# Seven products of quarters in the first feed-forward as well

## The chip, the cores and the metric

One NeuronCore of a Trainium2 chip runs the whole program. The metric is the device time of one execution in microseconds. PE is the TensorE engine (PEld its weight loads), DVE VectorE, ACT ScalarE, POOL GpSimd, SP the SyncE engine that issues most DMAs.

## What is computed

One block of a network on 256 tokens of width 2048, all in float32: a feed-forward, a mixer (S5 recurrence beside pooling), attention to a memory of 256 rows, and a second feed-forward. The part of the reference that the change touches is the two feed-forwards; the S5 tables and the norm of the memory only because their work is run beside the first.

```python
def rmsnorm(x, g):
    return x * rsqrt(mean(x * x, axis=-1, keepdims=True) + EPS) * g
def swiglu(x, w_gate, w_up, w_down):                   # 2048 -> 5632 -> 2048
    return (silu(x @ w_gate) * (x @ w_up)) @ w_down

h = h + 0.5 * swiglu(rmsnorm(h, g_ffn1), w1_gate, w1_up, w1_down)
...                                                    # mixer: s5_mixer(u_ssm, a, dt, b, c, ...), pool_mixer
memn = rmsnorm(mem, g_mem)
h = h + memory_cross_attention(rmsnorm(h, g_xattn), memn, w_q, w_k, w_v, w_o)
h = h + 0.5 * swiglu(rmsnorm(h, g_ffn2), w2_gate, w2_up, w2_down)
return rmsnorm(h, g_final)
```

## The kernel before

**Products.** A float32 weight tile is loaded as a 1 MB tile `raw` (128x4x512; pool `wraw`, three slots). `parts` (L137) splits it in two halves of 128x1024: ACT rounds the half to `whi` (L142), DVE subtracts to get `wlo` (L143). A pair of tiles whi and wlo comes from the pool `whl` with three slots; in the second feed-forward every second or third pair comes from another pool with two. The tokens are split in the same way (`xh`, `xl`). `tok_block` (L151 to L158) makes three 128x512 matmuls for each half of the tokens: xh by whi, xh by wlo, xl by whi. So a half-tile of weights feeds twelve matmuls, a tile 24.

**A chunk.** The 5632 inner columns are eleven chunks `f` of 512. A plain chunk is `tok_unit` (L163) over four tiles of gate and four of up, 192 matmuls in all; `gated` (L271) and `upped` (L282) make the product, `act_tiles` (L286) transposes and splits it for the down projection. These last steps are put on a list `late` and run at the next tile.

**The first feed-forward** (`ffn`, L294 to L339) runs the chunks in four passes (`PASSES`, L25), three chunks each and then two; after each pass come its four down tiles in width, each over the pass's chunks, and `add_to_h` (L258). All its chunks are plain. Beside it runs `aside` (L543 on), a generator with the tables of the S5 recurrence (`s5_tables`, L342 to L533: DVE products, PE transposes, writes of `Vd`, `WTd`, `Kd` to DRAM) and the sum of squares of the memory: 16 tiles `mem` of 128x256, each with a one-column memset on DVE (L550), a load that POOL issues (L551), a square on ACT (held in program order), and a sum into `ssm` on DVE (L202); the norm of it (`rnorm` L224, `spread` L215) goes into `Rm`. `step` (L299) advances the generator in five of every nine weight tiles, from the seventh on, so that it lasts through all eleven chunks; `mem` has six buffers.

**The second feed-forward** (L1006 on) runs chunks 0 and 1 plain and chunks 2 to 10 by `seven`: from quarters of the weights and of the tokens, seven products in place of eight. `product` (L1053 to L1062) makes 12 matmuls for a half product, with sums and differences of weight tiles (`less`, DVE operations of 128x512 x 2) and of tokens (`token_sums`: ten sums and differences on DVE, then SH on ACT and SL on DVE, in two `raw` slots). Such a chunk has 84 matmuls in `product` and 96 in `tok_block`, 180 in all, and more work on DVE and ACT than a plain one. Its buffers are in a pool `sw`. The down tiles of a pass are a generator `down`, which the chunks of the next pass advance. The first pass with seven products is pass 1.

What sets the order is program order on each engine; an engine runs its instructions one after the other, and a tile's slot that is not yet free holds the load or the memset that writes it, with all behind it. PSUM has eight banks: in the first feed-forward, the mixer and the attention pools of 6 and 2, in the second feed-forward 4 and 2, and two for the down tiles.

Of the kernel before, what the change touches and what calls it, by code (L numbers as in the profile page):

```python
# [23 lines left out]
PASSES2 = ((0, 2), (2, 4), (4, 6), (6, 8), (8, 10), (10, 11))  # L24
PASSES = ((0, 3), (3, 6), (6, 9), (9, 11))  # L25
# [29 lines left out]
def block_kernel(ctx: ExitStack, tc: tile.TileContext, xT, memT, wgu1, wd1, w_in, w_glu, w_pool, w_out,  # L55
# [10 lines left out]
    banks = ExitStack()  # L66
    psA = banks.enter_context(tc.tile_pool(name="psA", bufs=6, space=bass.MemoryType.PSUM))
    psB = banks.enter_context(tc.tile_pool(name="psB", bufs=2, space=bass.MemoryType.PSUM))
# [225 lines left out]
    def ffn(fe, wgu, wd, xs, aside=None, begin=None, before=None, after=None):  # L294


        calls = [0]

        def step():  # L299
            calls[0] += 1  # L300
            if aside is not None and calls[0] > 6 and calls[0] * 5 % 9 < 5:
                next(aside, None)

        late = []

        def held(more=None):
            def run(i):
                if i == 0:
                    while late:
                        late.pop(0)()  # L310
                if more is not None:
                    more(i)
                step()
            return run

        for a, b in PASSES:
            acts = []
            for f in range(a, b):
                if f == 0 and begin is not None:
                    ag, au = begin()  # L320
                else:
                    ag, au = tok_unit([cols4(wgu[4 * f:4 * f + 4, 0], i) for i in range(4)], xs, held(before if f == 0 else None)), None
                if f == 0:
                    ffn_norm()
                ss = gated(fe, ag)
                if au is None:
                    au = tok_unit([cols4(wgu[4 * f:4 * f + 4, 1], i) for i in range(4)], xs, held())
                upped(ss, au)
                late += [lambda ss=ss, t=t: act_tiles(ss, acts, t) for t in range(2)]
            for n in range(ND):  # L330
                more = None
                if b == FC and after is not None:
                    more = lambda i, n=n: after(n, i)
                add_to_h(tok_unit([cols4(wd[f, 4 * n:4 * n + 4], 0) for f in range(a, b)], acts, held(more)), n, qcol)
                if b == FC:
                    squares(n)
        if aside is not None:
            for _ in aside:
                pass  # L339

# [201 lines left out]
    with tc.tile_pool(name="pp", bufs=1) as pp, tc.tile_pool(name="fe1", bufs=2) as fe:  # L542
# [16 lines left out]
        def begin():  # L559
# [54 lines left out]
        ffn(fe, wgu1, wd1, xs, aside(), begin,  # L614
            after=lambda n, i: layer_in(xm, n - 1, G_MIX, [xp] * KT) if n > 0 and i == 1 else None)
# [393 lines left out]
    banks.close()  # L1009
    psA = ctx.enter_context(tc.tile_pool(name="psC", bufs=4, space=bass.MemoryType.PSUM))  # L1010
    psB = ctx.enter_context(tc.tile_pool(name="psD", bufs=2, space=bass.MemoryType.PSUM))
    fe = ctx.enter_context(tc.tile_pool(name="fe2", bufs=2))
    gate_up = lambda f, m: wgu2[4 * f:4 * f + 4, m]
    late = []

    def flush(n=2):
        for _ in range(min(n, len(late))):
            late.pop(0)()

    def finish_chunk(ss, acts):  # L1020
        late.extend([lambda t=t: act_tiles(ss, acts, t) for t in range(2)])

    def plain(f, acts, before=None):
        def first(i):
            flush()
            if before is not None:
                before(i)

        ag = tok_unit([cols4(gate_up(f, 0), i) for i in range(4)], xf, first)
        if f == 0:  # L1030
            ffn_norm()
        ss = gated(fe, ag, 2)
        upped(ss, tok_unit([cols4(gate_up(f, 1), i) for i in range(4)], xf))
        finish_chunk(ss, acts)

    def down(a, b, acts, accs_of=tok_accs, done=None):

        for n in range(ND):
            accs = accs_of()
            for i, f in enumerate(range(a, b)):  # L1040
                blocks = wtile(cols4(wd2[f, 4 * n:4 * n + 4], 0))
                flush()
                for j, w in enumerate(blocks):
                    tok_block(accs, w, acts[4 * i + j], i + j == 0, f == b - 1 and j == 3)
                if f == b - 1:
                    add_to_h(accs, n, qcol)
                    if done is not None:
                        done(n)
                yield

    def less(out, a, b):
        for c in (0, 256):
            V.tensor_tensor(out=out[:, :, c:c + 256], in0=a[:, :, c:c + 256], in1=b[:, :, c:c + 256], op=ALU.subtract)  # L1053

    def product(acc, w, x, first, last):

        acc = acc.rearrange("p (f c) -> p f c", f=4)
        for j, (wh, wl) in enumerate(parts(w)):
            xh, xl = x(j)
            T.matmul(acc, xh, wh, start=first and j == 0, stop=False)  # L1060
            T.matmul(acc, xh, wl, start=False, stop=False)  # L1061
            T.matmul(acc, xl, wh, start=False, stop=last and j == 3)  # L1062

    def quarter(k, lt):
        return lambda j: [xf[k + j][:, i * L + lt * P:i * L + (lt + 1) * P] for i in range(2)]

    with tc.tile_pool(name="sw", bufs=1) as sw:
        pairs[:] = [whl, sw, whl, sw, whl]
        SH = sw.tile([P, 4, 4, P], F32R, name="SH")
        SL = sw.tile([P, 4, 4, P], F32R, name="SL")  # L1070

        def token_sums():

            x = wraw.tile([P, 8, L], F32, name="raw")
            for k in range(8):
                V.tensor_tensor(out=x[:, k], in0=xf[k][:, :L].bitcast(F32), in1=xf[k][:, L:].bitcast(F32), op=ALU.add)
            q = [[x[:, 4 * i:4 * i + 4, lt * P:(lt + 1) * P] for i in range(2)] for lt in range(2)]
            s = wraw.tile([P, 4, 4, P], F32, name="raw")
            for o, a, b, op in ((0, q[1][0], q[1][1], ALU.add), (1, s[:, 0], q[0][0], ALU.subtract),
                                (2, q[0][0], q[1][0], ALU.subtract), (3, q[0][1], s[:, 1], ALU.subtract)):  # L1080
                V.tensor_tensor(out=s[:, o], in0=a, in1=b, op=op)
            for o in (0, 2):
                S.activation(out=SH[:, o:o + 2], in_=s[:, o:o + 2], func=AF.Copy)
                V.tensor_tensor(out=SL[:, o:o + 2], in0=s[:, o:o + 2], in1=SH[:, o:o + 2].bitcast(F32), op=ALU.subtract)

        def tsum(o):
            return lambda j: (SH[:, o, j], SL[:, o, j])

# [62 lines left out]
        for a, b in PASSES2:  # L1151
            acts = []
            for f in range(a, b):
                if f < 2:
                    plain(f, acts, (lambda i: layer_in(xf, ND - 1, G_FFN2, [xp] * KT) if i == 3 else None) if f == 0 else None)
                    if f == 0:
                        token_sums()
# [111 lines left out]
```

## Time and profile before

| | us |
|---|---|
| three runs | 2136.57, 2137.09, 2141.73 (median 2137.09) |
| profiled execution: its own time | 2138.39 |
| its span on the core | 2136.6 |
| PE busy | 2095.8 (98%) |
| PEld busy | 1731.6 (81%) |
| DVE busy | 1502.9 (70%) |
| ACT busy | 1077.2 (50%) |
| POOL busy | 141.5 (7%) |
| mean granted clock of PE | 0.995 |

The busy shares are means over stages with different limits. Matmuls are pipelined: a row's duration is longer than the distance to the next one. The rows of the trace below name an instruction by its line, engine and operation, the tile that it writes, the tiles that it reads, and the shapes.

### The profile page before, as it was taken

Reading aid. Unit: us, or ns where it says so; the run is one execution under the profiler, and the core shown is the slowest. Engines: PE = TensorE matmul, PEld = TensorE weight load, DVE = VectorE, ACT = ScalarE, POOL = GpSimd, SP = SyncE. Lnnn points to the kernel's source line nnn. Section 1 sums busy time; section 2 is a strip of 40 time slices with the busy share of each in tenths; the row PEclk is TensorE's granted clock in tenths of the full one; section 3 lists DMA queues with packets and bytes.
Section 4 is the critical chain, followed back from the end, with each engine's and each line's share of the span. In section 5 each row is a group of like instructions: output and inputs, shape, how many; then the busy total and the mean of one; then the engine's idle time right before and its main releaser. Section 6 shows DMA issues by size and latency. Waiting matters only on the chain.

```text
span 2136.6 us, 26778 instructions
## 1 busy us (share of the span) xinstructions
PE 2095.8 (98%) x10248; PEld 1731.6 (81%) x10248; DVE 1502.9 (70%) x2021; ACT 1077.2 (50%) x1510; POOL 141.5 (7%) x255
## 2 busy tenths in 40 slices
PE   8999999999999999979999999999999999999997
PEld 7888888888888888867888888888888888888885
DVE  5567776766656667836767755566888888888874
ACT  7443444344444555625655644544555555555553
POOL 0000011111110001840000000000000000000000
PEclk9999999999999999999999999999999999999999
DMA  7755777777776756868545556656665666565542
GB/s 239 216 182 193 214 212 222 215 223 221 217 225 185 233 196 220 263 202 246 190 161 178 196 179 210 203 166 225 181 198 178 193 210 209 181 201 187 183 155 96
DMA packets 202320, 427.58 MB, mean 200 GB/s; under 512 B 17872, under 2 KB 31376, under 8 KB 193104
## 3 DMA queue, kind: packets, MB, share of 16 engines
q1 hardware_dynamic: 181280, 392.35, 58.3%
q0 software_dynamic: 6416, 18.85, 3.0%
q10 hardware_dynamic: 14496, 14.68, 2.2%
q8 instruction: 80, 1.31, 0.2%
q14 instruction: 48, 0.39, 0.0%
HBM read 408.05 MB, written 16.78 MB: 199 GB/s over the span
## 4 chain that ended last, share of the span: by engine, by line
PE 92%; POOL 3%; DMA 2%; DVE 1%; ACT 1%; issue 1%; SPq 0%; DVEq 0%; ACTq 0%; POOLq 0%
PE acc L158 19%; PE acc L156 19%; PE acc L157 19%; PE acc L120 6%; PE dacc L156 3%; PE dacc L157 3%; PE dacc L158 3%; PE acc L121 3%; PE psb L1060 2%; PE psb L1062 2%; PE psb L1061 2%; PE acc L987 1%; PE acc L988 1%; PE acc L986 1%; PE acc L1062 1%; PE acc L1060 1%
## 5 line engine op out<-in xcount | busy, mean ns | idle before, releaser
L143 DVE TENSOR_TENSOR wlo<-raw,whi 128x1024 fp32r<-128x1024 f32 x522 | 636.3, 1224 | 362.7 <-ACT whi L142 357.8
L142 ACT ACTIVATE whi<-raw 128x1024 fp32r<-128x1024 f32 x522 | 553.4, 1061 | 644.8 <-PE acc L158 462.3
L157 PE MATMUL acc<-wlo,x 128*128 128x512 f32 x1760 | 689.7, 392 | 0.0
L158 PE MATMUL acc<-whi,x 128*128 128x512 f32 x1760 | 688.2, 392 | 0.0
L156 PE MATMUL acc<-whi,x 128*128 128x512 f32 x1760 | 637.7, 393 | 0.3 <-DVE h L262 0.3
L158 PEld LDWEIGHTS acc<-whi,x 128*128 128x128 f32 x1760 | 331.0, 188 | 70.6 <-issue 1.2
L157 PEld LDWEIGHTS acc<-wlo,x 128*128 128x128 f32 x1760 | 331.2, 188 | 70.1 <-issue 0.4
L156 PEld LDWEIGHTS acc<-whi,x 128*128 128x128 f32 x1760 | 330.5, 188 | 70.2 <-issue 1.1
L120 PE MATMUL acc<-x,whi 128*128 128x512 f32 x848 | 299.9, 399 | 3.1 <-ACT whi L100 3.1
L101 DVE TENSOR_TENSOR wlo<-raw,whi 128x1024 fp32r<-128x1024 f32 (+1 forms) x144 | 171.9, 1199 | 123.9 <-ACT whi L100 108.1
L121 PE MATMUL acc<-x,wlo 128*128 128x256 f32 x848 | 235.3, 283 | 2.8 <-DVE wlo L101 2.8
L100 ACT ACTIVATE whi<-raw 128x1024 fp32r<-128x1024 f32 (+1 forms) x144 | 146.8, 1023 | 153.5 <-PE acc L120 94.7
L120 PEld LDWEIGHTS acc<-x,whi 128*128 128x128 f32 x848 | 158.5, 188 | 41.4 <-ACT whi L100 5.2
L121 PEld LDWEIGHTS acc<-x,wlo 128*128 128x128 f32 x848 | 159.1, 189 | 8.3 <-DVE wlo L101 5.3
L158 PE MATMUL dacc<-whi,x 128*128 128x512 f32 x320 | 125.8, 394 | 0.0
L156 PE MATMUL dacc<-whi,x 128*128 128x512 f32 x320 | 124.9, 395 | 1.0 <-DVE h L264 1.0
L157 PE MATMUL dacc<-wlo,x 128*128 128x512 f32 x320 | 125.3, 391 | 0.0
L142 ACT ACTIVATE whi<-t 128x1024 fp32r<-128x1024 f32 x54 | 57.4, 1062 | 50.1 <-PE acc L158 30.1
L143 DVE TENSOR_TENSOR wlo<-t,whi 128x1024 fp32r<-128x1024 f32 x54 | 65.0, 1225 | 20.5 <-ACT whi L142 19.5
L143 DVE TENSOR_TENSOR wlo<-r,whi 128x1024 fp32r<-128x1024 f32 x54 | 65.9, 1220 | 15.1 <-ACT whi L142 15.1
L142 ACT ACTIVATE whi<-r 128x1024 fp32r<-128x1024 f32 x54 | 56.2, 1057 | 36.5 <-PE acc L158 15.0
L156 PEld LDWEIGHTS dacc<-whi,x 128*128 128x128 f32 x320 | 60.1, 188 | 14.0 <-issue 1.4
(276 smaller groups left out, 2135.3 us busy)
## 6 DMA issues: line engine op xcount, KB each, us to landing
raw<-in_wgu SPq DMA_DIRECT2D x148, 1024.0 KB, 6.1
raw<-in_wd SPq DMA_DIRECT2D x88, 1024.0 KB, 5.3
r<-in_wgu SPq DMA_DIRECT2D x27, 1024.0 KB, 6.1
raw<-in_w_in SPq DMA_DIRECT2D x16, 1024.0 KB, 5.0
raw<-in_w_k SPq DMA_DIRECT2D x16, 1024.0 KB, 5.3
raw<-in_w_out SPq DMA_DIRECT2D x32, 512.0 KB, 5.1
raw<-in_w_q SPq DMA_DIRECT2D x16, 1024.0 KB, 4.8
raw<-in_w_v SPq DMA_DIRECT2D x16, 1024.0 KB, 4.8
```

The lines of the kernel that those rows point to most:

```text
L100: S.activation(out=hi[:, :n], in_=r, func=AF.Copy)
L101: V.tensor_tensor(out=lo[:, :n], in0=r, in1=hi[:, :n].bitcast(F32), op=ALU.subtract)
L120: T.matmul(acc, w[0], x, start=first, stop=False)
L121: T.matmul(acc[:, :L], w[1], x[:, :L], start=False, stop=last)
L142: S.activation(out=hi, in_=raw[:, :, c:c + 256], func=AF.Copy)
L143: V.tensor_tensor(out=lo, in0=raw[:, :, c:c + 256], in1=hi.bitcast(F32), op=ALU.subtract)
L156: T.matmul(acc, xh, w[0], start=first, stop=False)
L157: T.matmul(acc, xh, w[1], start=False, stop=False)
L158: T.matmul(acc, xl, w[0], start=False, stop=last)
L1060: T.matmul(acc, xh, wh, start=first and j == 0, stop=False)
L1061: T.matmul(acc, xh, wl, start=False, stop=False)
L1062: T.matmul(acc, xl, wh, start=False, stop=last and j == 3)
```

## The change

The functions of the seven products move into `ffn`, which now serves both feed-forwards. In the first, chunks 5 to 10 use them (`SEVEN1`), in the second chunks 1 to 10 (`SEVEN2`). Both use the same passes: one chunk, then five of two chunks. So in the first feed-forward too the down tiles of a pass are run from within the next pass's chunks (`steps`), in accumulators `dacc` of their own, and its PSUM pools are 4 and 2 banks; the mixer and attention get 6 and 2 as before (`open_banks`). The side work `aside` is advanced by `tick` at each weight tile of the plain chunks 1 to 4, once and twice in turn. At chunk 5 `room` runs what is left of it, closes its pool `pp` and opens the pool `sw` of the seven products in the same memory; then come the token sums. In the second feed-forward the token sums stand at chunk 1, no longer within chunk 0. The code of `seven`, `product`, `less` and `token_sums` is the same as before apart from names.

```diff
-PASSES2 = ((0, 2), (2, 4), (4, 6), (6, 8), (8, 10), (10, 11))
-PASSES = ((0, 3), (3, 6), (6, 9), (9, 11))
+PASSES = ((0, 1), (1, 3), (3, 5), (5, 7), (7, 9), (9, 11))
+SEVEN1 = 5
+SEVEN2 = 1
...
+    psA, psB = open_banks(4)
...
+    def ffn(fe, wgu, wd, xs, seven_from, room, begin=None, before=None, tick=None):
+        gate_up = lambda f, m: wgu[4 * f:4 * f + 4, m]
+        todo = [iter(()), 0]
+
+        def steps(slot, slots=4):
+            flush()
+            for _ in range((slot + 1) * todo[1] // slots - slot * todo[1] // slots):
+                next(todo[0], None)
+
+        def plain(f):
+            def ahead(m):
+                def run(i):
+                    if i % 2 == 1 or todo[1] == 0:
+                        steps(2 * m + i // 2)
+                    if before is not None and f == 0 and m == 0:
+                        before(i)
+                    if tick is not None:
+                        tick()
+                return run
...
         for a, b in PASSES:
             acts = []
             for f in range(a, b):
...
+                if f == seven_from:
+                    sw = room()
+                    pairs[:] = [whl, sw, whl, sw, whl]
+                    SH, SL = (sw.tile([P, 4, 4, P], F32R, name=n) for n in ("SH", "SL"))
+                    token_sums()
+                ss = seven(f) if f >= seven_from else plain(f)
+                late.extend([lambda ss=ss, t=t, acts=acts: act_tiles(ss, acts, t) for t in range(2)])
+            for _ in todo[0]:
                 pass
+            if b < FC:
+                todo[0] = down(wd, a, b, acts, lambda: [psA.tile([P, 512], F32, name="dacc", bufs=2) for _ in range(2)])
+                n = next(y - x for x, y in PASSES if x == b)
+                todo[1] = ND * (b - a) // n
...
-        ffn(fe, wgu1, wd1, xs, aside(), begin,
-            after=lambda n, i: layer_in(xm, n - 1, G_MIX, [xp] * KT) if n > 0 and i == 1 else None)
+        def tick():
+            count[0] += 1
+            for _ in range(1 + (count[0] % 2)):
+                next(side, None)
+
+        def room():
+            for _ in side:
+                pass
+            spare.close()
+            return spare.enter_context(tc.tile_pool(name="sw", bufs=1))
+
+        for n, i in ffn(fe, wgu1, wd1, xs, SEVEN1, room, begin, tick=tick):
+            if n > 0 and i == 0:
+                layer_in(xm, n - 1, G_MIX, [xp] * KT)
+        spare.close()
+    psA, psB = open_banks(6)
...
+    units = ffn(fe, wgu2, wd2, xf, SEVEN2, lambda: spare.enter_context(tc.tile_pool(name="sw", bufs=1)),
+                before=lambda i: layer_in(xf, ND - 1, G_FFN2, [xp] * KT) if i == 3 else None)
```

**ACT where the tiles of mem begin.** Before, in the last chunks of the first feed-forward; `kr` is the last of the tables' work, `whi` a split of weights, `ssm` and `evq` the squares of mem.

```order
L529 ACTIVATE kr<-psb 128x128
L142 ACTIVATE whi<-raw 128x1024 x5
L198 ACTIVATE ssm<-mem 128x256
L142 ACTIVATE whi<-raw 128x1024 x4
L198 ACTIVATE evq<-mem 128x256 x2
```

After, at the end of chunk 4 and the entry to chunk 5:

```order
L203 ACTIVATE ssm<-mem 128x256
L147 ACTIVATE whi<-raw 128x1024 x2
L203 ACTIVATE evq<-mem 128x256 x15
L384 ACTIVATE SH<-raw 128x1024 x2
L147 ACTIVATE whi<-raw 128x1024 x2
L147 ACTIVATE whi<-t 128x1024 x2
```

The fifteen squares that stood in twos among the splits now stand in one row, ahead of the first split of chunk 5 (`SH` is the token sums' own rounding).

**DVE at the same places.** Before, one step of the side work among the splits:

```order
L264 SCALAR_TENSOR_TENSOR h<-acc,qcol,h 128x512 x2
L143 TENSOR_TENSOR wlo<-raw,whi 128x1024 x2
L550 MEMSET mem 128x1
L202 TENSOR_TENSOR ssm<-ssm,evq 128x256
...
L143 TENSOR_TENSOR wlo<-raw,whi 128x1024 x4
```

After, from the end of chunk 4 on (`s` and `h` are `upped` and a down tile's addition):

```order
L269 SCALAR_TENSOR_TENSOR h<-dacc,qcol,h 128x512 x2
L673 MEMSET mem 128x1 x5
L148 TENSOR_TENSOR wlo<-raw,whi 128x1024
L207 TENSOR_TENSOR ssm<-ssm,evq 128x256
...
L207 TENSOR_TENSOR ssm<-ssm,evq 128x256 x5
L235 TENSOR_SCALAR rv<-psb 128x2
```

The memsets of five tiles of mem (each of which lets POOL start a load) stand behind the addition to h; after one more split the sums and the other memsets follow in turn, fifteen sums in all, with no split among them, and the norm `rv` behind them.

**PE where it sums ssm over the partitions.** Before, within a plain tile:

```order
L156 MATMUL acc<-whi,x 128x512
L157 MATMUL acc<-wlo,x 128x512
L228 MATMUL psb<-ones,ssm 128x1 x2
L158 MATMUL acc<-whi,x 128x512
L156 MATMUL acc<-whi,x 128x512
```

After, in the last down tile `dacc` that is run before chunk 5:

```order
L163 MATMUL dacc<-whi,x 128x512
L233 MATMUL psb<-ones,ssm 128x1 x2
L161 MATMUL dacc<-whi,x 128x512 x2
L162 MATMUL dacc<-wlo,x 128x512
...
L161 MATMUL acc<-whi,x 128x512 x2
L162 MATMUL acc<-wlo,x 128x512
...
L226 MATMUL psb<-dg,ones 128x256
L329 MATMUL psb<-whi,x 128x512
```

The two matmuls on `ssm` now stand ahead of the last twelve of that down tile, of twelve into `acc` and of the first product of chunk 5 (L329); the column norm (`dg`) stands right before that product.

## Rows read from the trace of the kernel before

**Rows 1.** The page: busy time, share of the span, instructions of PE.

```profile
PE 2095.8 (98%) x10248; PEld 1731.6 (81%) x10248; DVE 1502.9 (70%) x2021; ACT 1077.2 (50%) x1510; POOL 141.5 (7%) x255
```

**Rows 2.** Windows of two stretches: busy us (count) by engine, granted clock, DMA.

```profile
core 0: us, PE busy (x) PEld busy (x) DVE busy (x) ACT busy (x) POOL busy (x), PEclk, DMA share, GB/s
640.00:700.00 60.00, 60.00 (x273) 49.73 (x272) 35.64 (x52) 28.18 (x36) 0.54 (x1) 1.00 0.66 193
1500.00:2050.00 550.00, 550.00 (x2424) 449.09 (x2423) 476.60 (x494) 298.74 (x326) 0.00 (x0) 1.00 0.62 192
```

**Rows 3.** Timeline of PE: start us, duration us, instruction; 57 matmuls apart.

```profile
640.09 0.39 PE L156 MATMUL acc<-whi,x 128*128 128x512 f32 x1
...
653.01 0.39 PE L156 MATMUL acc<-whi,x 128*128 128x512 f32 x1
```

**Rows 4.** Timeline of DVE in the first feed-forward, idle time before in brackets.

```profile
590.38 1.23 DVE L143 TENSOR_TENSOR wlo<-raw,whi 128x1024 fp32r<-128x1024 f32 x1 [1.49 <-ACT whi L142]
...
595.83 1.23 DVE L143 TENSOR_TENSOR wlo<-raw,whi 128x1024 fp32r<-128x1024 f32 x1 [1.49 <-ACT whi L142]
```

**Rows 5.** Groups on ACT: count, busy us, mean ns, idle before.

```profile
L142 ACT ACTIVATE whi<-raw 128x1024 fp32r<-128x1024 f32 x522 | 553.4, 1061 | 644.8 <-PE acc L158 462.3 <-PE dacc L158 84.7 <-PE psb L1062 23.4
```

**Rows 6.** Groups on DVE, same columns.

```profile
L143 DVE TENSOR_TENSOR wlo<-raw,whi 128x1024 fp32r<-128x1024 f32 x522 | 636.3, 1224 | 362.7 <-ACT whi L142 357.8 <-DMA Yd<-flip 1.4
L1053 DVE TENSOR_TENSOR t<-r,t 128x1024 f32<-128x1024 f32 x36 | 43.2, 1220 | 0.3
L264 DVE SCALAR_TENSOR_TENSOR h<-dacc,qcol,h 128x512 f32<-128x512 f32 x40 | 28.1, 744 | 0.4 <-PE dacc L158 0.4
L354 DVE TENSOR_TENSOR va<-va,w 128x576 f32<-128x576 f32 x16 | 12.0, 751 | 0.0
L202 DVE TENSOR_TENSOR ssm<-ssm,evq 128x256 f32<-128x256 f32 x15 | 6.3, 421 | 0.4
L212 DVE SCALAR_TENSOR_TENSOR ra<-ra,rv 128x2 f32<-128x2 f32 x24 | 3.8, 158 | 0.5
```

**Rows 7.** The tile mem: duration ns min/median/max, and time to landing.

```profile
L550 DVE MEMSET mem<- x16: 59/59/59, 562.6 to 646.0; 128x1 f32 x16
L551 POOL DMA_DIRECT2D mem<-in_memT x16: 537/539/575, 562.9 to 646.6; - x16
L198 ACT ACTIVATE evq<-mem x15: 401/401/405, 595.7 to 661.0; 128x256 f32<-128x256 f32 x15
DMA to landing us min/median/max: 5.1/5.6/6.2
```

**Rows 8.** Loads of like size (memk, kr), and weight loads on the page.

```profile
L619 SPq DMA_DIRECT2D memk<-in_memT x16: 327/334/597, 720.1 to 880.6; - x16
DMA to landing us min/median/max: 2.1/4.6/7.4
L532 POOL DMA_DIRECT2D Kd<-kr x32: 585/585/605, 272.0 to 574.5; - x32
DMA to landing us min/median/max: 2.4/2.9/5.2
raw<-in_wd SPq DMA_DIRECT2D x88, 1024.0 KB, 5.3
```

**Rows 9.** Timeline of DVE at the token sums of the second feed-forward.

```profile
1434.80 0.68 DVE L1081 TENSOR_TENSOR raw<-raw 128x512 f32<-128x512 f32 x1
...
1436.54 2.35 DVE L1084 TENSOR_TENSOR SL<-raw,SH 128x1024 fp32r<-128x1024 f32 x2
1444.05 2.36 DVE L143 TENSOR_TENSOR wlo<-raw,whi 128x1024 fp32r<-128x1024 f32 x2 [5.16 <-ACT whi L142]
```

**Rows 10.** Timeline and windows of PE around its longest stop.

```profile
934.74 0.69 PE L817 MATMUL psb<-tab,big 128*32 128x128 f32 x8 [11.65 <-DMA big<-big]
922.00:935.00 13.00, 1.34 (x13) 0.73 0.28 92
935.00:938.00 3.00, 3.00 (x50) 0.50 0.66 158
```

More of the change, by code (lines that the diff above doesn't have):

```diff
@@ L292, in act_tiles @@
             acts.append(split(ap_, pt[:, j]))
[L294 to L314, printed above, removed]
+    late = []
@@ new lines, in flush, with down @@
+    def flush():
+        while late:
+            late.pop(0)()
+    def down(wd, a, b, acts, accs_of=tok_accs, done=None):
+        for n in range(ND):
+            accs = accs_of()
+            for i, f in enumerate(range(a, b)):
+                blocks = wtile(cols4(wd[f, 4 * n:4 * n + 4], 0))
+                flush()
+                for j, w in enumerate(blocks):
+                    tok_block(accs, w, acts[4 * i + j], i + j == 0, f == b - 1 and j == 3)
+                if f == b - 1:
+                    add_to_h(accs, n, qcol)
+                    if done is not None:
+                        done(n)
+                yield n, i
@@ new lines, in less, with product @@
+    def less(out, a, b):
+        for c in (0, 256):
+            V.tensor_tensor(out=out[:, :, c:c + 256], in0=a[:, :, c:c + 256], in1=b[:, :, c:c + 256], op=ALU.subtract)
+    def product(acc, w, x, first, last):
+        acc = acc.rearrange("p (f c) -> p f c", f=4)
+        for j, (wh, wl) in enumerate(parts(w)):
+            xh, xl = x(j)
+            T.matmul(acc, xh, wh, start=first and j == 0, stop=False)
+            T.matmul(acc, xh, wl, start=False, stop=False)
+            T.matmul(acc, xl, wh, start=False, stop=last and j == 3)
@@ L318, in ffn @@
             for f in range(a, b):
[L319 to L338, printed above, removed]
-                pass
+                if f == seven_from:
[6 more added lines that the diff above has]
+            for _ in todo[0]:
+                pass
+            if b < FC:
+                todo[0] = down(wd, a, b, acts, lambda: [psA.tile([P, 512], F32, name="dacc", bufs=2) for _ in range(2)])
+                n = next(y - x for x, y in PASSES if x == b)
+                todo[1] = ND * (b - a) // n
+        pairs[:] = [whl]
+        return down(wd, *PASSES[-1], acts, done=squares)
     def s5_tables(pp):
@@ L1006, in block_kernel @@
     kp.close()
-    banks.close()
-    psA = ctx.enter_context(tc.tile_pool(name="psC", bufs=4, space=bass.MemoryType.PSUM))
-    psB = ctx.enter_context(tc.tile_pool(name="psD", bufs=2, space=bass.MemoryType.PSUM))
+    psA, psB = open_banks(4)
     fe = ctx.enter_context(tc.tile_pool(name="fe2", bufs=2))
[L1013 to L1062, printed above, removed]
@@ L1177, in columns @@
                     S.activation(out=o[:, k + j], in_=pt[:, j], func=AF.Copy, scale=vcol(G_FINAL + k + j))
-        for n, _ in enumerate(down(*PASSES2[-1], acts, done=squares)):
-            if n > 0:
+        for n, i in units:
+            if n > 0 and i == 0:
                 columns(n - 1)
```

184 lines of the change are left out of this document (90 added, 94 removed).

## The prediction

> **What bounds the kernel now.** I read the page first, then the share of each engine by stretch, then the order of PE's matmuls in time, and last the two places where PE waits. The reader is to see that PE is the bound almost everywhere: busy 98% of the span [rows 1], and in a stretch of the first feed-forward and one of the second busy in every microsecond at full clock [rows 2]. There a 128x512 matmul follows the last one after 12.92 us / 57 = 0.2267 us [rows 3] (its 0.39 us overlap). So a matmul less is worth 0.2267 us, if nothing else becomes late. The second stretch holds eight and a half chunks that already use the seven products, with DVE busy 476.6 of 550 us: dense, and without a gap on PE. In the first feed-forward DVE has 1.49 us of every 2.72 us (12 matmuls) to spare, because it waits for ACT, and ACT for a free pair of buffers [rows 4]. The lead is short there: three pairs of 2.72 us, less the one in use, less ACT's 1.06 [rows 5] and DVE's 1.22 us [rows 6], leave 3.2 us (an estimate) between the end of a split and its first matmul. Whatever holds DVE or ACT longer than that stops PE.
>
> **What it removes.** A plain chunk has 192 matmuls for gate and up, a seven-product chunk 84 + 96 = 180. Seven chunks change (six of the first feed-forward, chunk 1 of the second), so 84 matmuls go; the order of PE shows the same count. All are on the path: 84 x 0.2267 = **19.0 us** gained. The extra splits, differences and sums on DVE and ACT lie beside PE, as in the second stretch of [rows 2]; with that cover gone, each extra 128x1024 operation would cost its 1.22 us.
>
> **Chunks 1 to 4.** The S5 tables ran beside all eleven chunks; now DVE does them in four. By the new order DVE has in chunk 2 twenty splits (24.4 us), 30.0 us of table work (about forty operations near the 0.75 us of va [rows 6] and small ones) and 7.6 us of the rest: 62.1 us, against 58.9 us on PE (240 matmuls at 0.2267, 43 small ones at about 0.1). Chunks 3 and 4 have 63 and 65 us against some 68. Adding up row by row, with a lead of 3.2 us that cannot grow, PE waits 2.6 us in chunk 2 and nowhere else. Bounds: 0 (DVE at 87% hid everything in [rows 2]) and 6 us (three of the transposes are also late). I take **2.6**.
>
> **The entry to chunk 5** is where I expect the time to go. The side work is drained there, so 15 of the 16 tiles of mem for the norm of the memory come one behind the other: on ACT fifteen squares in a row, on DVE fifteen sums with their memsets, no split among them (in the order before, two squares stood between four splits). PE's next matmul after twelve of a down tile is the one that sums ssm over partitions, and it waits for the last of these sums. Step by step, from t0, the end of the last split of chunk 4:
> - PE has its lead 3.2 + 12 matmuls 2.7 = 5.9 us of work; then twelve matmuls (2.7) with a split that DVE does before the sums; then the ssm matmul.
> - DVE's next split needs a raw tile whose slot comes free only at t0: 5.3 us to landing [rows 8] + 1.06 of ACT + two signals of 0.1 = 6.6; the split 1.2; two additions to h 1.5 (these wait for PE's down tile, so no load of mem starts before it). The memsets that start the loads stand at t0 + 9.3.
> - A load: 0.3 from memset to its DMA [rows 7], then to landing. There it took 5.1 to 6.2 us, but each time a 1 MB weight load had just been issued. In the new order SyncE's queue is stuck behind the load of r12, which waits for the old room, so no weights move. Near rows of the same size: 2.1 at the least for memk and 2.4 to 2.9 for Kd [rows 8]. I take 2.6; ends 2.1 and 5.6. Then square 0.40, sum 0.42 [rows 7, 6], signals 0.4: 4.1 us for the first tile.
> - Six buffers: the memset for tile k+5 stands behind the sum of tile k. Fifteen tiles are three rounds: 4.1 + 2 x 4.2 + four more sums at 0.55 (POOL's 0.54 a load) = 14.7 us. The sums end at t0 + 24.0.
> - DVE then has, before the split for PE's third half-tile from here, 13 operations of 1.22 us (SL, differences, splits) and nine small ones of 0.16 [rows 6]: 17.4 us, so t0 + 41.4. In between PE has only 14 matmuls, 3.2 us.
> PE's own work in that time is 5.9 + 2.7 + 3.2 = 11.8, so it stands still for **29.6 us**. Cheapest: loads of 2.1 us and the raw tile there in time give 25.6. Dearest: loads of 5.6 us, three rounds, 38.6.
> The Trainium skill ("DMA: Bandwidth & Descriptors", section on the anatomy of one DMA on the gpsimd path) puts a DMA at about 2.0 us plus its bytes over 436 GB/s, an estimate of 2.3 us for these 128 KB. The trace's 5.1 to 6.2 us disagree with it, behind weight loads; no run shows the quiet case yet. By the rule the three rounds are 0.9 us shorter and the sum is 18.8 us of loss instead of 19.7; by the loaded row it is 28.7.
>
> **The clock** after it: PE's one long stop, 11.65 us, was followed by a granted clock of 0.50 for the 3 us from 935 on, and 1.00 later [rows 10]; matmuls there run at 1.2 GHz, so 3.8 us of work cost some 1.9 us more. Two stops, the first partly inside the second: **2.5 us**, bounds 0 and 5.
>
> **Chunk 1 of the second feed-forward.** The token sums now stand right before their first use. In the trace DVE idled 5.16 us there, and the next split came 8.6 us after the raw slot was last read [rows 9]; a whole plain chunk hid it. Now the product r11, with two halves of 1.4 us of matmuls, comes next, and two differences stand before its first split: 7.3 us landing, 2.4 of differences, 1.4 of the gate, 1.2 split is 12 to 13 us against 2.7 plus a lead of 3 to 8 us; then two more short waits. **4 us**, bounds 0 and 8. Its 2.7 us of gain is in the 19.0.
>
> **At nothing:** from the first feed-forward's last down units to the second's chunk 0 the rows on DVE, ACT, POOL and SP are the same. Re-laid PSUM banks cost at most one accumulator's eviction (0.74 us [rows 6]); the last pass with two chunks only moves four down tiles, at 2.4 us of DVE under 5.4 us of PE each.
>
> **The sum**, against the profiled execution (2138.39 us; span 2136.6): -19.0 + 2.6 + 29.6 + 2.5 + 4.0 = +19.7, so 2158.1. It lies 1.3 above the median of the three runs, so I forecast **2157 us**.
>
> **Rivals.**
> - *Faster: the entry is hidden.* One mechanism: PE is not held by the sums, since the loads of mem land while PE still has work, as at the second feed-forward's entry, where DVE's 5.16 us cost PE nothing. Then -19.0 + 2.6 + 4.0 = -12.4: 2125. It decides this way if the stop at chunk 5 is under 6 us (faster by 0.3% up to 12.4 less 6.4). Against: the additions to h tie the loads to PE's own last matmul, and 17.4 us of DVE come after the sums. Chance 0.08.
> - *No change.* All low ends: 25.6 with no clock loss and covers elsewhere: +6.6, 2143 or a little less. 0.09.
> - *Loads as slow as in the trace before* (5.6 us): 9 us more, 2166. Writes of tables, or the weights of r12, would have to move at the same time. 0.18.
> - *Tables crowd DVE* through chunks 2 to 4, with the writes of Vd, WTd and Kd holding it too (va waits for its last write; 20 us a round instead of 41): 10 us more, 2167. 0.12.
> That the matmuls don't go is excluded by the order's counts.
>
> **How the numbers follow.** My forecast's own case (2145 to 2165) has 0.53. Slower by over 0.3% (6.4 us, about what measurement can tell from no change): 0.53 + 0.18 + 0.12 = 0.83. Within: 0.09. Faster: 0.08. The range leaves out the faster case, the lower half of no change and a little above: 2143 to 2172.
>
> **What would show it.** Right: in the first feed-forward a stop of PE of some 20 us about 300 us in, released by DVE's sum of ssm, and one of about 9 us released by a split soon after; fifteen squares in a row on ACT; the clock at 0.50 behind them; small waits in chunk 2 and at chunk 1 of the second feed-forward; seven chunks 2.7 us shorter elsewhere. Wrong: no stop over 6 us there, or loads of mem that land at 5 us, or a DVE that idles in chunks 1 to 4.

## The result and the profile after

The changed kernel takes 2171.40 us (median of four runs, 2169.97 to 2173.56), the kernel before in its four 2136.83: a ratio of 1.0165 (1.0153 to 1.0177), so slower by some 35 us. The profiled execution took 2169.97 us with a span of 2167.7, 31.1 more than before. PE's busy time shows nothing of it, against [rows 1]:

```profile
PE 2096.8 (97%) x10164; PEld 1719.6 (79%) x10164; DVE 1660.2 (77%) x2205; ACT 1130.5 (52%) x1568; POOL 141.7 (7%) x255
```

84 matmuls are gone (10164 records in place of 10248), and PE's busy time rose by 1.0 us. Cut at the first matmul of the mixer and at that of the second feed-forward, as their starts stand in the trace, the two spans are:

| stage, us | before | after | moved | forecast |
|---|---|---|---|---|
| first feed-forward | 760.8 | 783.6 | +22.8 | +18.4 |
| mixer and attention | 447.1 | 446.8 | -0.3 | 0 |
| second feed-forward | 928.7 | 937.2 | +8.5 | +1.3 |

(The forecast's first line is -16.3 for 72 matmuls, +2.6, +29.6, +2.5; its third -2.7 and +4.0.) So the direction and the largest piece came out, and 11 us are missing, 4 in the first and 7 in the second feed-forward. These are stages of one trace each, and a stage with the same code is not the same to the microsecond: over all kernels below, mixer and attention take between 444.2 and 452.6 us, and the first matmul of the first feed-forward starts at 8.26 us before and at 6.65 us after, so that from there on its stage moved by 24.4 us.

**The entry to chunk 5** is where the forecast put it. The five largest waits of PE from 300 to 365 us (what waited, for what; us in total, times, longest):

```profile
PE psb L233 <- DVE ssm L207: 9.2, 1, 9.2
PE acc L161 <- ACT whi L147: 5.8, 1, 5.8
PE dacc L161 <- ACT whi L147: 4.1, 1, 4.1
PE dacc L161 <- DVE mem L673: 3.1, 1, 3.1
PE dacc L162 <- DVE wlo L148: 1.3, 2, 0.8
```

That is 23.5 us, the longest piece released by DVE's sum of ssm. DVE, start and duration, from the memsets to the last sums of mem:

```profile
318.17 0.09 DVE L673 MEMSET mem<- 128x1 f32 x5
...
331.88 0.95 DVE L207 TENSOR_TENSOR ssm<-ssm,evq 128x256 f32<-128x256 f32 x2 [0.51 <-ACT evq L203]
```

The sums ended 14.7 us after the memsets (332.8 - 318.2), which is the forecast's number. The loads landed as in the quiet case, not as in [rows 7] (issue to landing of the tile mem):

```profile
DMA to landing us min/median/max: 2.4/2.4/3.4
```

The forecast took 2.6. The Trainium skill's rule ("DMA: Bandwidth & Descriptors", anatomy of one DMA on the gpsimd path: about 2.0 us plus bytes over 436 GB/s, an estimate of 2.3 us here) is borne out by this row, since no weights moved: SyncE issued nothing between these two rows (start, us):

```profile
309.48 0.37 SPq L154 DMA_DIRECT2D raw<-in_wd  x1
333.98 1.47 SPq L154 DMA_DIRECT2D r<-in_wgu  x3
```

What came after the sums was sized nearly right (17.2 us from their end to PE's third half-tile, 17.4 in the forecast), but its releaser was another one. Behind the queue's release three 1 MB tiles and soon two more were loaded at once, and PE's last stop ended with ACT, whose raw tile had just landed, not with DVE's work. Start, us, instruction, idle before; the last row is ACT's:

```profile
332.89 1.01 PE L233 MATMUL psb<-ones,ssm 128*128 128x1 f32 x4 [9.17 <-DVE ssm L207]
...
341.00 0.63 PE L162 MATMUL dacc<-wlo,x 128*128 128x512 f32 x1
...
342.70 0.63 PE L163 MATMUL dacc<-whi,x 128*128 128x512 f32 x1
...
350.04 1.22 PE L161 MATMUL acc<-whi,x 128*128 128x512 f32 x2 [5.83 <-ACT whi L147]
348.93 1.06 ACT L147 ACTIVATE whi<-raw 128x1024 fp32r<-128x1024 f32 x1 [5.36 <-DMA raw<-in_wgu]
```

Between the second and the third row lie four matmul distances in 1.70 us, 0.425 us each: half speed. Windows of the same stretch (busy us (count) of PE, PEld, DVE, ACT, POOL; then the granted clock, DMA share, GB/s):

```profile
314.00:324.00 10.00, 6.13 (x18) 3.96 (x16) 5.85 (x18) 4.20 (x7) 4.09 (x8) 0.83 0.43 149
324.00:340.00 16.00, 2.23 (x7) 1.45 (x7) 10.08 (x29) 7.90 (x14) 3.99 (x8) 0.58 0.52 162
340.00:352.00 12.00, 6.14 (x14) 4.12 (x15) 11.25 (x15) 3.18 (x3) 0.00 (x0) 0.64 1.04 388
352.00:365.00 13.00, 12.73 (x55) 9.85 (x54) 7.30 (x9) 7.10 (x11) 0.00 (x0) 0.93 0.35 101
```

The granted clock is below 1.00 in all four windows, 51 us; [rows 10] had shown 0.50 (of the levels 1.2 and 2.4 GHz the lower) for 3 us behind one stop. From the starts in the trace some 24 matmuls ran at half speed there: 24 x 0.2 = 4.8 us in place of 2.5. Stops and clock together are 28.3 us, against 32.1 forecast.

**What is missing in the first feed-forward** is in no wait. From 365 to 780 us the view of waits is empty for PE, and it is busy in every microsecond (window of PE: us, busy (count), clock, DMA share, GB/s):

```profile
400.00:740.00 340.00, 340.00 (x1502) 1.00 0.60 188
```

The starts tell it: in this stretch a 128x512 matmul follows the last one after 230.5 ns on the mean (distances under 245 ns, so without stops), where the plain chunks of before have some 227. Runs of twelve that stay near 226.7 change with runs near 233.

**The second feed-forward.** PE around chunk 1 and the start of chunk 2:

```profile
1470.58 0.50 PE L329 MATMUL psb<-whi,x 128*128 128x512 f32 x1 [1.46 <-ACT whi L147]
1472.47 0.33 PE L295 MATMUL psb<-ident,s 128*128 128x128 f32 x1 [1.38 <-DVE s L289]
...
1481.07 0.50 PE L162 MATMUL acc<-wlo,x 128*128 128x512 f32 x1 [1.03 <-DVE wlo L148]
...
1538.09 0.67 PE L162 MATMUL acc<-wlo,x 128*128 128x512 f32 x1 [2.55 <-DVE wlo L148]
```

DVE at the same places, where it has to wait for the load of r11 both times:

```profile
1469.39 2.36 DVE L322 TENSOR_TENSOR t<-r,raw 128x1024 f32<-128x1024 f32 x2 [3.11 <-DMA raw<-in_wgu]
...
1516.95 2.36 DVE L322 TENSOR_TENSOR t<-r,raw 128x1024 f32<-128x1024 f32 x2 [2.57 <-DMA raw<-in_wgu]
```

The share of DVE in chunk 1 (first row; us, busy by PE, PEld, DVE, ACT, POOL), and in a stretch of seven products of the kernel before (second fence):

```profile
1470.00:1536.00 66.00, 60.62 (x258) 47.83 (x258) 60.53 (x64) 37.26 (x42) 0.00 (x0) 0.97 0.62 199
```

```profile
1480.00:1546.00 66.00, 66.00 (x293) 53.85 (x292) 53.58 (x55) 35.37 (x39) 0.00 (x0) 1.00 0.58 176
```

60.5 of 66 us against 53.6: chunks 1 and 2 have half the down tiles beside them (the pass before has one chunk), so fewer matmuls that cover the same splits and differences. The two waits for r11 are the largest slack that DVE has (5.7 us; 2.7 more go to PE and ACT), so that little is left to catch up what it loses. That this makes the stop at chunk 2 is tested below (e8).

### The profile page after: what moved, and what is told of

Read it like the earlier page. It is cut to its first block, busy times and chain, and to the rows that moved or that the text cites. A ratio compares the mean times of both kernels' runs of the same rounds, so it can differ in the third digit from the quotient of the medians.

```text
span 2167.7 us, 26868 instructions
## 1 busy us (share of the span) xinstructions
PE 2096.8 (97%) x10164; PEld 1719.6 (79%) x10164; DVE 1660.2 (77%) x2205; ACT 1130.5 (52%) x1568; POOL 141.7 (7%) x255
## 4 chain that ended last, share of the span: by engine, by line
PE 88%; POOL 3%; DVE 3%; DMA 3%; issue 1%; ACT 1%; SPq 0%; DVEq 0%; ACTq 0%; POOLq 0%
PE acc L162 13%; PE acc L163 13%; PE acc L161 13%; PE acc L125 7%; PE dacc L161 6%; PE dacc L162 6%; PE dacc L163 6%; PE acc L126 3%; PE psb L329 3%; PE psb L331 3%; PE psb L330 3%; PE acc L331 2%; PE acc L329 2%; PE acc L330 2%; PE acc L1127 1%
## 5 line engine op out<-in xcount | busy, mean ns | idle before, releaser
L148 DVE TENSOR_TENSOR wlo<-raw,whi 128x1024 fp32r<-128x1024 f32 x480 | 582.5, 1221 | 171.7 <-ACT whi L147 166.2
L162 PE MATMUL acc<-wlo,x 128*128 128x512 f32 x1280 | 504.0, 394 | 4.3 <-DVE wlo L148 3.8
L163 PE MATMUL acc<-whi,x 128*128 128x512 f32 x1280 | 502.4, 393 | 0.0
L161 PE MATMUL acc<-whi,x 128*128 128x512 f32 x1280 | 466.5, 395 | 6.1 <-ACT whi L147 5.8
L162 PEld LDWEIGHTS acc<-wlo,x 128*128 128x128 f32 x1280 | 241.5, 189 | 59.2 <-DVE wlo L148 5.3
L161 PEld LDWEIGHTS acc<-whi,x 128*128 128x128 f32 x1280 | 240.5, 189 | 58.5 <-ACT whi L147 6.5
L163 PEld LDWEIGHTS acc<-whi,x 128*128 128x128 f32 x1280 | 241.5, 189 | 52.1 <-issue 0.4
L161 PE MATMUL dacc<-whi,x 128*128 128x512 f32 x576 | 222.0, 397 | 7.7 <-ACT whi L147 4.5
L162 PE MATMUL dacc<-wlo,x 128*128 128x512 f32 x576 | 227.5, 395 | 1.3 <-DVE wlo L148 1.3
L163 PE MATMUL dacc<-whi,x 128*128 128x512 f32 x576 | 228.0, 396 | 0.0
L148 DVE TENSOR_TENSOR wlo<-t,whi 128x1024 fp32r<-128x1024 f32 x96 | 115.7, 1223 | 50.3 <-ACT whi L147 49.5
L148 DVE TENSOR_TENSOR wlo<-r,whi 128x1024 fp32r<-128x1024 f32 x96 | 117.1, 1220 | 25.6 <-ACT whi L147 24.5
L161 PEld LDWEIGHTS dacc<-whi,x 128*128 128x128 f32 x576 | 108.3, 189 | 31.2 <-issue 4.4
```

The costliest lines, as they stand in the source:

```text
L148: V.tensor_tensor(out=lo, in0=raw[:, :, c:c + 256], in1=hi.bitcast(F32), op=ALU.subtract)
L161: T.matmul(acc, xh, w[0], start=first, stop=False)
L162: T.matmul(acc, xh, w[1], start=False, stop=False)
L163: T.matmul(acc, xl, w[0], start=False, stop=last)
```

## The experiments

Theory A at the start: the drained sums of mem make the stop at chunk 5; the token sums before their use make that in the second feed-forward. Rivals: the entry is dear by itself; the tables crowd DVE; the second feed-forward loses by the jump to seven products one chunk earlier. Each ratio is against the kernel before as it was timed with that kernel (five medians for it, 2135.76 to 2136.74).

**e1_no_mem**

```diff
-            for k in range(KT + 4): ...      # loads, squares, sums of mem, rnorm, spread
+            V.memset(rmcol, 1.0)
+            V.memset(Rm, 1.0)
```

> The changed kernel without the sum of squares of the memory (its loads, squares, sums and norm are left out; rmcol and Rm are set to 1). Theory A (the stop at chunk 5 is the fifteen squares and sums run in a row): PE's stops at the entry to chunk 5 fall from 23.5 us idle (31 us with the slow clock behind them) to under 8 us, the time to 2145 to 2150 us. Rival B (the entry is dear by itself: token sums, the pool that is opened in the old one's room, loads held until then): 15 us or more stay, the time is 2160 or above. Unlike the other runs it also saves some 9 us of DVE work, which PE does not wait for.

Measured: 2145.68 us (ratio 1.0041, 1.0026 to 1.0055). PE's waits from 300 to 365 us fall to 3.9 us, the longest 1.5. Theory A.

**e4_tick_2**

```diff
-            for _ in range(1 + (count[0] % 2)):
+            for _ in range(2):
```

> The changed kernel with two steps of the side work at each tile of chunks 1 to 4 in place of one and a half, so that the squares of the memory fall among the splits of chunk 4 and nothing is left at chunk 5. Theory A (the drain is the cause): the entry to chunk 5 costs 8 us or less in place of 31, DVE's denser chunks 1 to 4 cost 0 to 5, the time is 2147 to 2154 us. Rival B (DVE has no room for it: what is no longer drained is waited for within chunks 1 to 4): 2162 us or above. Rival C (the entry is dear by itself): 2160 to 2170 with the stop still at chunk 5.

Measured: 2145.15 us (1.0041, 1.0027 to 1.0056), 26 less than the changed kernel, with all the work in it; that is a little under theory A's range. PE's waits from 300 to 360 us are now only these:

```profile
PE psb L330 <- DVE wlo L148: 1.7, 2, 1.1
PE psb L295 <- ACT s L404: 0.6, 1, 0.6
```

With weight loads moving beside them the tiles of mem land as late as in [rows 7] and not after the 2.4 us of the drained entry, and PE does not wait for it:

```profile
DMA to landing us min/median/max: 3.2/6.2/7.9
```

So the stop was the drain. But the first feed-forward is 758.5 us here, 2.3 less than before the change, where 72 matmuls are worth 16.3; where the rest goes is added up in the next part.

**e3_plain_1**

```diff
-SEVEN1 = 5
+SEVEN1 = 11          # and the side work is run out before its pool closes
```

> The changed kernel with no seven products in the first feed-forward (SEVEN1 = 11; new passes, tables within chunks 1 to 4 and all of the second feed-forward as in the changed kernel; the squares of the memory then follow in chunk 5 and 6 by the tick). Theory A (tables in four chunks cost under 3 us; the loss of the first feed-forward is the entry, 31 us, and a slower pitch of matmuls in the chunks of seven products, 4 to 6 us): 72 matmuls come back (+16.3 us), 35 to 37 us go, so 2150 to 2153 us. Rival B (crowding in chunks 1 to 4 or the new passes cost 10 us or more): 2158 or above.

Measured: 2149.08 us (1.0061, 1.0040 to 1.0083). Theory A. The first feed-forward takes 764.1 us, 3.3 more than before with the same matmuls: that is what the tables in four chunks and the new passes cost as far as one trace tells, without a single wait of PE from 60 to 420 us. The forecast had 2.6, as a stop in chunk 2; there is none in the changed kernel either.

**e2_sums_in_0**

```diff
             ss = gated(fe, ag, 2)
+            if f == seven_from - 1 and tick is None:
+                open_seven()                 # pool sw, SH, SL, token_sums()
             upped(ss, au or ...)
```

> The changed kernel, with the token sums and the pool of the second feed-forward back within chunk 0, behind its gate, as before the change; seven products still from chunk 1 on. Theory A (token sums right before their use cost PE 11 us there, 2.6 of them at the next chunk as an after-effect): the second feed-forward gets 8 to 11 us shorter, the time is 2160 to 2163 us. Rival B (what costs is the jump to seven products at chunk 1, whose first tiles r11 and r12 have less time, whatever the sums do): it stays within 3 us of 2171.

Measured: 2168.07 us (1.0149, 1.0129 to 1.0169); the second feed-forward 932.5 us in place of 937.2. The changed second feed-forward is the same in e1, e3 and e4, where it takes 937.1, 936.3 and 934.7 us, so the place of the sums is worth 2 to 5 us. That is between the two theories; the whole time moved by 3 us, and the two intervals overlap. Chunk 2's stop of 2.0 us stays. Theory A was too simple.

**e7_ffn2_before** and **e8_few_less**, both on top of e4_tick_2:

```diff
+PASSES2 = ((0, 2), (2, 4), (4, 6), (6, 8), (8, 10), (10, 11))    # e7, second feed-forward
-SEVEN2 = 1
+SEVEN2 = 2                                                       # e7, sums within chunk 0
...
+            if not few:                                          # e8, chunks 1 and 2
                 less(t, r22, t)                                  # so too less(r12, ...), less(t, r21, t)
```

> e4_tick_2 with the second feed-forward as before the change (seven products from chunk 2 on, two chunks in its first pass, token sums within chunk 0). Theory A (of the changed second feed-forward chunks 1 and 2 are bound by DVE: half the down tiles beside them, 228 matmuls or 51.7 us of PE against some 50 us of DVE and the 8.5 us of the sums): the second feed-forward takes 929 us from its first matmul, as before the change, in place of 934 to 937, the time is 2138 to 2141 us. Rival B (it is slower for another reason, as the pools of PSUM or where the buffers lie): 2143 or above.

> e4_tick_2 with three of the four differences of weight tiles left out in chunks 1 and 2 of the second feed-forward (six operations of 1.22 us on DVE in each; the products then use the wrong weights). Theory A (DVE is the bound in these two chunks): the stop of 2.3 us at the start of chunk 2 with its slow clock goes, and part of chunk 1's stops: 2139 to 2142 us. Rival B (late loads of r11 and r12 bound them): 2144 to 2147, the stops stay.

Measured: e7 2138.80 us (1.0006, 0.9997 to 1.0015), its second feed-forward 928.7 us as before the change. e8 2142.39 us (1.0024, 1.0015 to 1.0034), between its two theories; it is 2.8 us under e4, with intervals that overlap, so the waits have to decide. The largest waits of PE from 1430 to 1550 us, e4_tick_2 first, then e8:

```profile
PE acc L162 <- DVE wlo L148: 2.9, 2, 2.1
PE psb L295 <- DVE s L289: 1.7, 2, 1.4
PE psb L329 <- ACT whi L147: 1.4, 1, 1.4
```

```profile
PE psb L295 <- DVE s L289: 1.7, 2, 1.4
PE psb L329 <- ACT whi L147: 1.5, 1, 1.5
```

With less work on DVE chunk 2's stop (2.1 us, on wlo) is gone; chunk 1's stops stay as they were. So chunk 2's is DVE's. That chunk 1's is the late first tile is read from DVE's wait for r11 above; no run moved that load alone.

**e5_whl_only** and **e6_pad**, for the pitch, both on top of e4_tick_2. The moving operands of the seven products come from pairs in whl and in sw in turn, so the place was the first suspect.

```diff
-                    pairs[:] = [whl, sw, whl, sw, whl]           # e5: left out
...
+                    sw.tile([P, 96], F32, name="pad")            # e6: first tile of sw, 384 bytes
                     pairs[:] = [whl, sw, whl, sw, whl]
```

> e4_tick_2 with the split weights of the seven products in the pool whl alone (three pairs in place of five; the pool sw keeps its other tiles). In the chunks of seven products a matmul follows the last one after 230.4 ns on the mean, in plain chunks after 226.7. Theory A (the slow ones are those that read a pair in sw): the pitch falls to 227 to 228 ns in both feed-forwards, which is worth 14 to 16 us, and what the shorter lead costs stands against it: 2130 to 2150 us. Rival B (the pitch belongs to the chunk's work, dense DVE and ACT, wherever the pairs are): the pitch stays at 230 and stops are added, 2150 us or above.

> e4_tick_2 with 384 bytes of padding ahead of the pairs in sw, so that they start at the same offset within 512 bytes as those of whl (before: 128 bytes further). If the offset makes their matmuls slow, the pitch in the chunks of seven products falls from 230.4 to 227 to 228 ns and the time by 14 to 16 us, to 2130; if not, nothing changes: 2144 to 2147 us.

Measured: e5 2185.42 us (1.0225, 1.0190 to 1.0260); the mean distance fell only to 228.7 ns and stops came in both feed-forwards (17 of them, 28.3 us, for wlo at one line), so three pairs are too short a lead, and the pairs are not the whole cause. e6 2132.81 us (0.9975, 0.9963 to 0.9987), 12.3 less than e4 by 384 unused bytes; the distance is 226.9 ns in both feed-forwards, and the first takes 752.4 us, 6.1 less than in e4.

**e9_before_pad, e12_before_pad_pairs, e13_before_pad_128, e14_before_pad_256**: the same on the kernel before, whose second feed-forward has the slow pitch too.

```diff
+        sw.tile([P, 96], F32, name="pad")        # e9; e13: 32 elements, e14: 64
         pairs[:] = [whl, sw, whl, sw, whl]
         SH = sw.tile(...)
         SL = sw.tile(...)
+        sw.tile([P, 96], F32, name="pad")        # e12, in place of the one above
...
+            if f == 2:                           # e12: behind the pairs, so that the rest keeps its place
+                sw.tile([P, 32], F32, name="pae")
```

> The kernel before the change with 384 bytes of padding ahead of the tiles of its pool sw (second feed-forward), nothing else. If the offset of sw within 512 bytes is what makes the matmuls of the seven products slow (230 ns a matmul against 226.7, in the kernel before as well), the second feed-forward gets 8 to 10 us shorter: 2126 to 2129 us. If e6_pad owed its 12 us to something of the changed kernel alone, nothing changes: 2135 to 2138.

> The kernel before with only the pairs of split weights in sw moved by the 384 bytes; SH, SL and the other tiles of sw keep their offsets. Theory A (PE is slow where its moving operand lies at the other offset): as e9_before_pad, 2126 to 2129 us and a pitch of 227. Rival B (SH and SL, PE's other operand, or the tiles that DVE reads and writes make it slow): a part of the gain at most, 2131 to 2137 us.

> The kernel before with 128 bytes of padding ahead of its pool sw in place of 384. With 384 the tiles of sw start at 352 within 512 bytes, like those of whl and of the tokens (before at 480). With 128 they start at 96 within 512, which is the same as whl within 256 bytes, but not within 512. If what counts repeats every 256 bytes, the pitch is 226.8 ns as with 384 and the time 2126 to 2129 us; if it repeats every 512, the pitch stays at 229 to 230 and the time at 2133 to 2138.

> The same with 256 bytes: the tiles of sw start at 224 within 512, so 224 within 256 bytes, as without padding. If what counts repeats every 256 bytes, nothing changes: 230 ns, 2133 to 2138 us; if it is something else, the pitch moves.

The tiles of sw in the built programs, the time, and the mean distance of matmuls from 1510 to 2060 us:

| kernel | start of sw's tiles, bytes within 512 (256) | us | ratio | ns |
|---|---|---|---|---|
| before | 480 (224) | 2136.83 | 1 | 230.2 |
| e9 | 352 (96) | 2127.32 | 0.9956 (0.9941 to 0.9971) | 226.8 |
| e13 | 96 (96) | 2126.50 | 0.9948 (0.9929 to 0.9968) | 226.8 |
| e14 | 224 (224) | 2136.47 | 0.9999 (0.9987 to 1.0010) | 230.2 |
| e12 | pairs 352 (96), others 480 (224) | 2129.86 | 0.9966 (0.9954 to 0.9978) | 228.3 |

e12 lies between its two theories. Windows from 1500 to 2050 us of e13 and e14, in this order; the row of before is in [rows 2], with 2424 matmuls, and those of e9 and e12 have 2459 and 2445:

```profile
1500.00:2050.00 550.00, 550.00 (x2459) 455.42 (x2458) 480.84 (x498) 303.86 (x329) 0.00 (x0) 1.00 0.62 194
```

```profile
1500.00:2050.00 550.00, 550.00 (x2424) 449.14 (x2423) 475.92 (x492) 299.08 (x325) 0.00 (x0) 1.00 0.61 192
```

Every one of them is "busy 550 of 550 at clock 1.00"; the count alone differs. In e12, which splits the two operands, the starts tell which of them counts (five distances from the first row to the second, ten from the third to the fourth):

```profile
1542.44 0.40 PE L1060 MATMUL acc<-whi,SH 128*128 128x512 f32 x1
...
1543.60 0.39 PE L1062 MATMUL acc<-whi,SL 128*128 128x512 f32 x1
...
1579.28 0.39 PE L156 MATMUL acc<-whi,x 128*128 128x512 f32 x1
...
1581.54 0.39 PE L157 MATMUL acc<-wlo,x 128*128 128x512 f32 x1
```

1.16 us / 5 = 232 ns where SH and SL (still at 224) are one operand, 2.26 / 10 = 226 where pairs and tokens are both at 96. So a tile at 224 can make the matmul slow as either operand. But 224 alone does not. By the starts in the built program of the kernel before, the last product of a chunk makes six matmuls of SH and SL with a pair of sw, both at 224, and then six with a pair of whl, at 96. The first and the last start of each six there:

```profile
1542.52 0.39 PE L1060 MATMUL acc<-whi,SH 128*128 128x512 f32 x1
...
1543.66 0.39 PE L1062 MATMUL acc<-whi,SL 128*128 128x512 f32 x1
1543.89 0.40 PE L1060 MATMUL acc<-whi,SH 128*128 128x512 f32 x1
...
1545.05 0.39 PE L1062 MATMUL acc<-whi,SL 128*128 128x512 f32 x1
```

Over the nine chunks of seven products the first six follow at 227.5 ns here and at 232.8 in e12, the second six at 232.5 and 233.6: moving the pair from 224 to 96 made the first six slow. What these rows share is that matmuls are slow where the two tiles start at different places within 256 bytes. Whether two tiles at 224 are always fast is open: the other two sixes of this kind in a chunk stand among slow ones and take some 232 ns. The Trainium skill ("SBUF — State Buffer", operand start alignment) asks of an operand only that it starts at a multiple of its element size, and every start here is one; these rows show that the time of a matmul depends on more.

**e10_after_pad**

```diff
+                    sw.tile([P, 96], F32, name="pad")            # the changed kernel, nothing else
```

> The changed kernel with the padding alone. The prediction took 226.7 ns for each matmul of the new chunks. If the pitch was the term that it lacked, the time falls by 12 to 15 us to 2157 to 2160 us, and what is left above the kernel before are the stops at chunk 5 and in the second feed-forward. Rival: with the long stop at chunk 5 in it the padding gives less than 6 us, 2165 or above.

Measured: 2160.07 us (1.0108, 1.0093 to 1.0123), 11 less than without the pad, at the edge of what the theory gave. Its window, against the 1502 above:

```profile
400.00:740.00 340.00, 340.00 (x1525) 1.00 0.61 191
```

**e11_e7_pad and e15_e7_pad_all**: e7_ffn2_before with the pad in sw, and with 128 bytes behind the small pool ev in its place, which moves the pools behind it by as much, sw from 224 to 96.

```diff
+    ev.tile([P, 32], F32, name="pad", bufs=1)                     # e15
```

> e7_ffn2_before (two side steps at each tile, second feed-forward as before the change) with the padding in both feed-forwards. Theory: the slow pitch is worth 6 us in the first feed-forward and 9 in the second, so 2138.8 less 15, 2122 to 2126 us, against the kernel before faster by 0.5 to 0.7%. Rival (stops take up what the pitch gives, as DVE has to keep up with a faster PE): 2130 or above.

> e7_ffn2_before with 128 bytes of padding behind the small pool that lies ahead of fe1, fe2, sw and the pools of the mixer and the attention, so that all of these start at 96 within 256 bytes, as wraw, whl and the tokens do (in every kernel so far they start at 224). If the rule of e13 and e14 holds for any matmul's operands, the feed-forwards gain what e11_e7_pad gained, and the matmuls of the mixer and the attention that read tiles there may gain 1 to 4 us more: 2120 to 2125 us. If the seven products' pool was the only place where it counts, 2124 to 2126, as e11_e7_pad.

Measured: e11 2124.63 us (0.9939, 0.9924 to 0.9954), e15 2121.56 us (0.9931, 0.9914 to 0.9948). Both beat both kernels. They were not timed side by side and their intervals overlap; mixer and attention take 446.3 and 446.4 us in the two traces. A further gain there is not shown.

## Why the prediction was right and wrong

Two steps failed. The pace of the new chunks was taken from a plain chunk, so that their slower one was in no term (6.1 us); and the entry to seven products in the second feed-forward was put at 4 us, where it took 9 to 11. The mechanism of the largest term, the entry to chunk 5, was right.

- **84 matmuls, 19.0 us:** right in count, and in worth as far as sums tell. In e4 the first feed-forward gains 2.3 us: 16.3 for 72 matmuls, less 3.3 (e3), 6.1 (the pitch, below) and 4.7 of short stops that its trace still has is 2.2. In e11, without the pitch, it gains 6.3 (754.5 against 760.8): 16.3 less 3.3 and 5.8 of stops is 7.2.
- **The entry to chunk 5, 29.6 + 2.5 us:** right in place, cause and size: 23.5 of stops, 4.8 of clock, and e4 and e1 take 26 us away with the cause. Inside it, the sums took the 14.7 us. The forecast's own steps stop PE for 15.4 us up to their end and for 14.2 behind it, and not for the "some 20" and "about 9" of its last paragraph; the trace has 12.8 and 10.7, the latter released by late weights, and the clock twice as dear. With 3.3 (e3) and the 6.1 below, -16.3 + 28.3 + 3.3 + 6.1 = 21.4 of the 22.8 us are accounted for (of 24.4 by the first matmul's start); the rest is open.
- **Chunks 1 to 4, 2.6 us:** the size was near (3.3 in e3), the mechanism was not: no stop anywhere, but small losses spread over the chunks, which these runs don't resolve further.
- **Chunk 1 of the second feed-forward, 4 us:** mis-sized; it came to 8.5 + 2.7 = 11.2 in this trace, and to 8.7 by that of e4. PE's stops from 1430 to 1550 us are 8.5 us, and the slow clock behind them some 2.6 more. 2 to 5 of it hang on the place of the sums (e2). The step that failed is "then two more short waits": it asked what chunk 1 waits for, and not how full DVE is once half the down tiles beside it are gone. Chunk 2's stop and the slow clock behind it were in no term; e7, with the old passes, loses nothing.
- **The term that was not there:** the first paragraph set "a matmul less is worth 0.2267 us" from [rows 3], in a plain chunk, and read the second row of [rows 2] as the same pace "without a gap". It was not: the new chunks run at 230.5 ns. 276 matmuls in each of six chunks, 1656 x 3.7 ns (230.5 less 226.8) = 6.1 us, nearly all in the first feed-forward, since the second had them already but for chunk 1, which adds under 1 us (226.8 is the distance with the pad, and e6 against e4 has the same 6.1 us in that stage). The trace of before held the number: fifty-seven starts in the second stretch would have shown it.
- **The rivals:** loads of 5.6 us and crowded tables did not come true; the time came near theirs (2166, 2167) for other reasons. With the pitch taken out, the first feed-forward of e10 is 779.9 us, 19.1 above before where the forecast had 18.4; the measured pieces without the pitch add up to 15.3, so this closeness is in part luck as well. That e10's whole time, 2160.07, lies 3 us from the forecast is luck: the pad also gives the second feed-forward 9 us that it had lost before the change (e9: 919.0 us there, e10: 927.8), which hides what chunks 1 and 2 cost.

## What to carry to other kernels

Before work that ran beside a loop is squeezed into fewer turns, look at what is run out at the seam: fifteen small operations in a row on two engines, with the loads behind them, cost more than the whole change could bring, and one number (the step's rate) mends it. Take the price of an operation from the stage that it will stand in, by the distance of starts: a full busy share at full clock hid 1.6% here. And where a stage of dense work begins earlier, ask which cover it had there.

## What the runs showed of the hardware

A 128x512 float32 matmul pays 6 to 7 ns more (233 in place of 226.7) when of its two tiles, moving and stationary, one starts at 224 within 256 bytes of the partition and the other at 96. Sorted by the starts of both tiles, the matmuls of the kernel before with six alike in front of them follow at 226.9 ns where both are at 96 (4356 of them), and at 232.8 and 233.1 where the stationary or the moving one is at 224 (69 and 386). A shift of sw by 128 or by 384 bytes takes the difference away, one of 256 does not. Two tiles at 224 were fast in one place of each chunk and not in others; other starts than these two, and why, are open. It is worth 9 to 10 us of the kernel before, for 128 unused bytes. Second, five stops of 0.8 to 9.2 us within 35 us left matmuls between them at 0.425 us apiece, 4.8 us in all: a stop's price is not its idle time alone, and several short ones cost more clock here than the 1.9 us that the forecast worked out for one of 11.65 us.
